# Moving low parts, modulation and the last rows' additions between the engines of a fused transformer layer

## The chip, the cores and the metric

The kernel runs on one core of a Trainium2 chip. Five engines work side by side, each through its own list of instructions in order: TensorE (PE, products; its weight loads are shown as PEld), VectorE (DVE), ScalarE (ACT), GpSimd (POOL) and SyncE (SP, which only issues transfers). ACT and POOL can issue transfers too. The metric is the time of one execution on the device in microseconds (us); less is better.

## The reference

One layer with latent tokens x (1024 x 1024), 256 context tokens, and adaLN modulation from a conditioning vector. Cut to what is computed:

```python
mod = silu(c) @ w_ada + b_ada                 # shift, scale, gate of both sub-layers
h = modulate(rms_norm(x, g_pre_mix), sh_m, sc_m)          # the context likewise
u_f, q_a, kv_a, kr_raw = split(h @ w_in)                  # 512, 256, 128, 32 columns
attn = mla_attention(q, k, v)      # from rms_norm(q_a) @ w_q_b, rms_norm(kv_a) @ w_kv_b, rotary parts
four = fourier_mix(u_f, w_fourier) # real 2-D DFT over positions and channels, then a map per group
x = x + gt_m * rms_norm(concat(four, attn) @ w_out, g_post_mix)
h2 = modulate(rms_norm(x, g_pre_ffn), sh_f, sc_f)
x = x + gt_f * rms_norm((silu(h2 @ w_gate) * (h2 @ w_up)) @ w_down, g_post_ffn)
```

All of it is in float32.

## The kernel before

**Products.** A float32 product is made of three products of a shorter type: each operand is split into a high part (a rounded copy) and a low part (what the copy leaves), and high x high, high x low and low x high are added up (`mm3_steps`, L68 to L70). `split` (L45) writes the high part on ACT (L50) and the low part on DVE (L56, "v") or on GpSimd (L58, "p"). Every operand that is split in the kernel passes through one ACT instruction and one DVE or GpSimd instruction of the same size.

**Order.** The kernel is written as one program; a tile scheduler sorts the instructions of each engine by when it thinks their inputs are there, and gives buffers in the order of the program. Where a few instructions are pinned (`pin`), their written order is kept. The order on an engine is so a result of the whole program, and can change where nothing is edited.

**Stages.** Constants (L167): 83 rows of 128 (c, c_ctx, gains, b_ada) are loaded and transposed into `cols`. `first_tiles` (L217): for each of eight slices j of the channels, a *set*, it loads the slice of w_ada (`araw`, 1 MB in two loads), splits it in two halves (`ah`, `al`, 128x1024 each), multiplies it with the conditioning vectors (16 products `aps`, L253 and L254), copies the result row (`arow`, L256), turns it into columns (`cps`, L259), forms `SH` and `A` (L261, L262), modulates two transposed tiles of x (`h`, L264), splits `h` (`hh`, `hl`), and adds 12 products with the slice of `w_in` to two accumulators (L290). The slice of w_in (`wraw`, 128x928) is split into `win`. The program puts modulation j + 2 ahead of the products of j. The tiles of x come through `normed` (L198): load (L202, two slots `xs`), square with sum (L86), rstd (L76, L78 on GpSimd), scaling in place on GpSimd (L204), then eight transposes on PE (L209). The third tile's transposes stand inside the last sets. `other_tiles` then takes the other tiles of x and the context: `h` for eight slices by ACT (L321, in a group of five and one of three around a split), products L345.

The Fourier stage (DFT over positions and channels) carries the weights of the attention beside it: `attention_weights` (L546) scales w_q (two tiles, 128x1024), w_k and w_v by gains and splits them (`wqh` and `wql`, and so on), splits the compressed keys (`kvTh`, `kvTl`) and the rotary keys `kr32` (32x1280) into K0. The first tile of w_q is scaled on GpSimd (L575) and split with its low part there; the second goes through `weight` (L567 on ACT scales into the high part, L568 on DVE makes the low part in one instruction). `wfpair`, `chh` and `chl` are the parts of w_fourier and the channel table; the products `mps` make a map from them, which is split into `map0` and `map1`.

After attention, output projection, gate and up, `down` (L1112) ends the kernel. Eight rows of 128 tokens finish one after the other: PE's last products of a row come into a bank, DVE adds them (L1190), ACT takes the square sum (L86) and adds the first half's (L1210), GpSimd raises to the power -1/2 (`rstd`, L1212). `finish` (L1164) is called for the row before: for rows 0 to 6 DVE multiplies by rstd and the gate row `Gf` (L1170), and GpSimd issues a store that adds to what lies in the output (x1, written there earlier); for row 7 x1 is loaded into a tile ahead of time, Gf is multiplied in early (L1205, L1209), DVE multiplies by rstd and adds x1 in halves (L1175), and the halves are stored plainly from SP and ACT (L1176).

## Time and profile before

| | |
|---|---|
| median of 3 runs | 1302.64 us (1301.27 to 1303.33) |
| profiled run | 1300.21 us |
| its span | 1298.4 us |
| granted clock, mean | 0.982 |
| PE busy | 1222.3 us, 94% |
| PEld (weight loads, beside PE) | 955.1 us, 74% |
| DVE busy | 934.2 us, 72% |
| ACT busy | 633.5 us, 49% |
| POOL busy | 479.4 us, 37% |
| chain that ended last | PE 49%, ACT 2%, POOL 2%, DVE 1%, DMA 1% |
| loaded and stored | 181.64 MB, 140 GB/s over the span |

Times in the trace are microseconds from the start of the span. The profiled run is one execution; its own time is the span and 1.8 us around it. A busy PE isn't a PE at its peak: products are pipelined, and their ends are modelled. Idle time ahead of an instruction is put down to what ended it, in brackets, by the last of its semaphores.

### The profile page before, as it was taken

Reading aid. Unit: us, or ns where it says so; the run is one execution under the profiler, and the core shown is the slowest. Engines: PE = TensorE matmul, PEld = TensorE weight load, DVE = VectorE, ACT = ScalarE, POOL = GpSimd, SP = SyncE. Lnnn points to the kernel's source line nnn. Section 1 sums busy time; section 2 is a strip of 40 time slices with the busy share of each in tenths; the row PEclk is TensorE's granted clock in tenths of the full one; section 3 lists DMA queues with packets and bytes.
Section 4 is the critical chain, followed back from the end, with each engine's and each line's share of the span. In section 5 each row is a group of like instructions: output and inputs, shape, how many; then the busy total and the mean of one; then the engine's idle time right before and its main releaser. Section 6 shows DMA issues by size and latency. Waiting matters only on the chain.

```text
span 1298.4 us, 15437 instructions
## 1 busy us (share of the span) xinstructions
PE 1222.3 (94%) x5474; PEld 955.1 (74%) x5474; DVE 934.2 (72%) x1301; ACT 633.5 (49%) x1045; POOL 479.4 (37%) x333
## 2 busy tenths in 40 slices
PE   5899978979999999889999999999999999999995
PEld 4588866756666666668788888888888887888884
DVE  6866586687675765353689887777777875898795
ACT  5467747646757668255644444433444433221232
POOL 4365556434555453253263332333311300000173
PEclk9999989989999999999999999999999999999998
DMA  8375211011110104642125554434454468987537
GB/s 318 127 246 169 69 49 36 31 33 46 38 33 17 34 18 139 179 140 101 60 81 179 178 178 149 150 110 144 163 178 154 153 212 335 344 296 256 194 130 130
DMA packets 79369, 181.64 MB, mean 140 GB/s; under 512 B 9569, under 2 KB 41332, under 8 KB 79292
## 3 DMA queue, kind: packets, MB, share of 16 engines
q1 hardware_dynamic: 67228, 137.89, 31.8%
q10 hardware_dynamic: 10800, 39.06, 7.7%
q0 software_dynamic: 1264, 3.70, 1.8%
q8 instruction: 43, 0.70, 0.2%
q14 instruction: 34, 0.28, 0.1%
HBM read 129.15 MB, written 51.48 MB: 139 GB/s over the span
## 4 chain that ended last, share of the span: by engine, by line
PE 49%; issue 2%; ACT 2%; POOL 2%; DVE 1%; DMA 1%; POOLq 0%; DVEq 0%; SPq 0%; ACTq 0%
PE gu L69 10%; PE gu L70 10%; PE gu L68 10%; PE y L774 5%; PE dn L68 4%; PE dn L70 4%; PE dn L69 4%; DMA unit<-zu 1%; DMA raw<-w_down 1%; POOL T L58 0%; POOL out_dram L1171 0%; PE T L209 0%; ACT H L321 0%; POOL rstd L1212 0%; DVE rows L1170 0%
## 5 line engine op out<-in xcount | busy, mean ns | idle before, releaser
L50 ACT ACTIVATE unit<-raw 128x512 fp32r<-128x512 f32 x171 | 105.5, 629 | 226.2 <-PE gu L70 106.3
L58 POOL TENSOR_TENSOR pl<-p,ph 128x1024 fp32r<-128x1024 f32 x53 | 128.8, 2431 | 148.0 <-ACT ph L50 111.6
L56 DVE TENSOR_TENSOR unit<-raw,unit 128x512 fp32r<-128x512 f32 x171 | 149.3, 881 | 27.3 <-ACT unit L50 26.9
L715 DVE TENSOR_REDUCE mx<-sps 128x1 f32<-128x512 f32 (+1 forms) x192 | 105.5, 594 | 31.5 <-PE sps L714 30.6
L640 ACT ACTIVATE p<-S 128x1024 f32<-128x1024 f32 x80 | 81.7, 1022 | 87.1 <-PE S L637 76.6
L935 POOL TENSOR_TENSOR s<-raw 128x512 f32<-128x512 f32 x22 | 33.8, 1537 | 241.4 <-DMA raw<-w_gate 167.9
L1155 POOL TENSOR_TENSOR rows<-rows,acc 128x512 f32<-128x512 f32 x8 | 13.5, 1705 | 212.8 <-DVE acc L1138 211.5
L50 ACT ACTIVATE ph<-p 128x1024 fp32r<-128x1024 f32 x80 | 84.3, 1057 | 1.9
L69 PE MATMUL gu<-T,unit 128*128 128x512 f32 x176 | 69.4, 394 | 0.9 <-POOL T L58 0.9
L70 PE MATMUL gu<-Bh,unit 128*128 128x512 f32 x176 | 69.4, 394 | 0.5 <-DVE unit L56 0.5
L68 PE MATMUL gu<-Bh,unit 128*128 128x512 f32 x176 | 69.4, 394 | 0.0
L69 PE MATMUL gu<-Bl,unit 128*128 128x512 f32 x176 | 69.3, 394 | 0.0
L70 PE MATMUL gu<-T,unit 128*128 128x512 f32 x176 | 69.3, 393 | 0.0
L68 PE MATMUL gu<-T,unit 128*128 128x512 f32 x176 | 69.2, 393 | 0.0
L68 PE MATMUL dn<-unit 128*128 128x512 f32 x148 | 58.2, 393 | 0.4 <-ACT unit L50 0.4
L70 PE MATMUL dn<-unit 128*128 128x512 f32 x148 | 58.0, 392 | 0.0
L69 PE MATMUL dn<-unit 128*128 128x512 f32 x148 | 58.0, 392 | 0.0
L621 PE MATMUL O<-pl,Vh 128*65 128x512 f32 x160 | 53.3, 403 | 4.6 <-POOL pl L58 3.8
L345 PE MATMUL acc<-win,hh 128*128 128x512 f32 (+1 forms) x224 | 55.8, 368 | 0.9 <-ACT hh L50 0.6
L1083 DVE TENSOR_TENSOR u<-u,gu 128x512 f32<-128x512 f32 x66 | 44.8, 681 | 15.6 <-PE gu L70 15.0
L78 POOL TENSOR_TENSOR rstd<-var,mhalf 128x1 f32<-128x1 f32 x44 | 27.6, 629 | 76.3 <-DVE var L76 75.6
L774 PE MATMUL y<-woh,xth 128*128 128x512 f32 x128 | 52.5, 410 | 2.4 <-ACT xth L50 2.4
(425 smaller groups left out, 3552.9 us busy)
## 6 DMA issues: line engine op xcount, KB each, us to landing
zu<-zpair ACTq DMA_DIRECT2D x50, 512.0 KB, 4.3
unit<-zu SPq DMA_DIRECT2D x47, 512.0 KB, 4.6
adraw<-w_ada SPq DMA_DIRECT2D x32, 512.0 KB, 3.9
units<-zu SPq DMA_DIRECT2D x27, 512.0 KB, 5.5
zu<-zone ACTq DMA_DIRECT2D x24, 512.0 KB, 3.1
raw<-w_gate SPq DMA_DIRECT2D x22, 512.0 KB, 4.2
raw<-w_up SPq DMA_DIRECT2D x22, 512.0 KB, 6.3
raw<-w_down SPq DMA_DIRECT2D x22, 512.0 KB, 5.2
```

The lines of the kernel that those rows point to most:

```text
L50: nc.scalar.activation(hi, src, AF.Copy)
L56: self.lastv = nc.vector.tensor_tensor(lo, src, hi.bitcast(F32), ALU.subtract)
L58: nc.gpsimd.tensor_tensor(lo, src, hi.bitcast(F32), ALU.subtract)
L68: self.nc.tensor.matmul(out, ah, bh, start=i == 0, stop=False)
L69: self.nc.tensor.matmul(out, ah, bl, start=False, stop=False)
L70: self.nc.tensor.matmul(out, al, bh, start=False, stop=i == n - 1)
L345: nc.tensor.matmul(acc[:, o], a[:, k, :], b[:, k, c], start=k == 0 and n == 0, stop=k == KT - 1 and n == 2)
L621: nc.tensor.matmul(O[0:m, ns], a, b[:, ns], start=k == 0 and i == 0, stop=k == NK - 1 and i == 2)
L640: nc.scalar.activation(p32, S, AF.Exp, scale=SCALE)
L715: nc.vector.tensor_reduce(mx[:, i, c:c + 1], ps[:, 0:n], AX.X, ALU.max)
L774: nc.tensor.matmul(ps[:, ns], u[:, k, :], w[:, k, ns], start=k == 0 and i == 0, stop=k == KT - 1 and i == 2)
L1083: V(d, d, ps, ALU.add)
```

## The change

- `normed` takes a queue; the first two tiles of x are loaded from ACT's queue instead of SP's. The third and later tiles stay on SP.
- In `first_tiles` the low part of w_in goes from GpSimd to DVE; the copy `arow` and the modulation `h` go from DVE to ACT.
- In the Fourier stage the low parts of w_fourier, the channel table and the rotary keys go from GpSimd to DVE; the first tile of w_q goes through `weight`, as the second does, so that the scaling on GpSimd (L575) is gone.
- The rows of constants are padded with zeros from 83 to 96.
- At the end x1 is loaded ahead for rows 4 to 7 (four loads instead of one). For these rows the product with Gf is made on DVE into accumulators that are free by then (L1193 of the changed kernel), DVE multiplies by rstd and adds x1 in one instruction, and the store is plain, from SP (row 7 in halves, from SP and ACT). Rows 0 to 3 keep the adding store of GpSimd. `finish` is called after the power of the row instead of before it.

```diff
--- before.py
+++ after.py
@@ -167,7 +167,7 @@
     def constants(self):
         tc, nc, t, cst = self.tc, self.nc, self.t, self.cst
         rows = cst.tile([P, P], F32, name="rows")
-        nc.sync.dma_start(rows[0:NROWS, :], t["rows"])
+        nc.sync.dma_start(rows[0:96, :], t["rows"])
         self.ident = cst.tile([P, P], F32, name="ident")
         nc.sync.dma_start(self.ident, t["ident"])
         self.comb = cst.tile([4, 2], F32, name="comb")
@@ -195,11 +195,11 @@
         self.Gm = cst.tile([P, D], F32, name="Gm")
 
 
-    def normed(self, src):
+    def normed(self, src, queue=None):
 
         nc = self.nc
         xs = self.xp.tile([P, D], F32, name="xs", bufs=2)
-        nc.sync.dma_start(xs, src)
+        (queue or nc.sync).dma_start(xs, src)
         r = self.rstd(self.xp, self.meansq(self.xp, xs, D))
         nc.gpsimd.tensor_scalar(xs, xs, r, 0.0, ALU.mult, ALU.add)
         return xs
@@ -228,10 +228,10 @@
             raw = sw.tile([P, 928], F32, name="wraw", bufs=3)
             nc.sync.dma_start(raw, t["w_in"][j * P:(j + 1) * P, :])
             wh, wl = (w[:, j, :] for w in self.win)
-            self.split(wh, wl, raw, "a", "p")
+            self.split(wh, wl, raw, "a", "v")
             return wh, wl
         xT = sw.tile([P, KT, 2 * P], F32, name="xT")
-        xs = [self.normed(t["x"][i * P:(i + 1) * P, :]) for i in range(2)]
+        xs = [self.normed(t["x"][i * P:(i + 1) * P, :], nc.scalar) for i in range(2)]
         raw = ada_load(0)
         nc.sync.dma_start(self.comb, t["comb"])
         for i in range(2):
@@ -253,7 +253,7 @@
                 nc.tensor.matmul(ps[0:4, 0:256], self.c4[:, k, :], ah[:, k, :], start=k == 0, stop=False)
                 nc.tensor.matmul(ps[0:4, 0:256], self.c4[:, k, :], al[:, k, :], start=False, stop=k == KT - 1)
             row = sw.tile([4, 256], F32, name="arow", bufs=2)
-            nc.vector.tensor_copy(row, ps[0:4, 0:256])
+            nc.scalar.activation(row, ps[0:4, 0:256], AF.Copy)
             ps = self.bankB("cps")
             for i in range(2):
                 nc.tensor.matmul(ps[:, 2 * i:2 * i + 2], row[:, i * P:(i + 1) * P], self.comb, start=True, stop=True)
@@ -261,7 +261,7 @@
             nc.vector.tensor_scalar(self.SH[:, :, j], ps[:, 0:2], self.cols[:, b0:b0 + 1], None, ALU.add)
             nc.vector.tensor_scalar(self.A[:, :, j], ps[:, 2:4], self.b1[:, 8 + j:9 + j], self.cols[:, R_GPM + j:R_GPM + j + 1], ALU.add, ALU.mult)
             h = sw.tile([P, 2 * P], F32, name="h", bufs=2)
-            nc.vector.tensor_scalar(h, xT[:, j, :], self.A[:, 0, j:j + 1], self.SH[:, 0, j:j + 1], ALU.mult, ALU.add)
+            nc.scalar.activation(h, xT[:, j, :], AF.Identity, bias=self.SH[:, 0, j:j + 1], scale=self.A[:, 0, j:j + 1])
             hh = sw.tile([P, 2 * P], F32R, name="hh", bufs=3)
             hl = sw.tile([P, 2 * P], F32R, name="hl", bufs=3)
             self.split(hh, hl, h, "a", "v")
@@ -521,8 +521,8 @@
         pair = fp.tile([P, 2, 512], F32R, name="wfpair")
         wfh, wfl = pair[:, 0, :], pair[:, 1, :]
         chh, chl = (fp.tile([P, 2, P], F32R, name=f"ch{x}") for x in "hl")
-        self.split(wfh, wfl, wf, "a", "p")
-        self.split(chh, chl, ch, "a", "p")
+        self.split(wfh, wfl, wf, "a", "v")
+        self.split(chh, chl, ch, "a", "v")
         run(positions(0))
         self.last_turn(bank)
         run(weights)
@@ -568,16 +568,11 @@
             nc.vector.scalar_tensor_tensor(w[1], raw, self.cols[:, g:g + 1], w[0].bitcast(F32), ALU.mult, ALU.subtract)
         weight(self.wk, rawk, R_GKV)
         for k in range(2):
-            w = [w[:, k, :] for w in self.wq]
-            if k:
-                weight(w, raws[k], R_GQ + k)
-            else:
-                nc.gpsimd.tensor_scalar(raws[k], raws[k], self.cols[:, R_GQ + k:R_GQ + k + 1], 0.0, ALU.mult, ALU.add)
-                self.split(*w, raws[k], "a", "p")
+            weight([w[:, k, :] for w in self.wq], raws[k], R_GQ + k)
             self.split(*(x[:, k, :] for x in self.qT), self.q32[:, k, :], "a", "v")
         yield
         self.split(*self.kvT, self.kv32, "a", "v")
-        self.split(kh[64:96, :], kl[64:96, :], self.kr32[64:96, :], "a", "p")
+        self.split(kh[64:96, :], kl[64:96, :], self.kr32[64:96, :], "a", "v")
         weight(self.wv, rawv, R_GKV)
         yield
 
@@ -910,8 +905,8 @@
             for j in range(2):
                 for p in group:
                     yield self.raw((p, "w", j), t["w_down"][(2 * p + j) * P:(2 * p + j + 1) * P, :])
-        i = NT - 1
-        yield self.raw(("x1", i), t["out"][i * P:(i + 1) * P, :])
+        for i in range(NT // 2, NT):
+            yield self.raw(("x1", i), t["out"][i * P:(i + 1) * P, :])
 
     STEPS = [(m, i) for ms in ((1, 2), (6, 5), (7,), (3,), (4,)) for m in ("w_gate", "w_up") for i in ms]
     DOWN = (1, 2, 6, 5, 7, 3, 4)
@@ -1158,7 +1153,9 @@
         last = NF // 2 - 1
         ss = {}
         pin = self.tc.keep_in_program_order
-        rows = [x[:, q].rearrange("p h c -> p (h c)") for x in (up, low) for q in range(4)]
+
+        rows = [up[:, q].rearrange("p h c -> p (h c)") for q in range(4)]
+        rows += [a[n][:, q:q + 2].rearrange("p q c -> p (q c)") for n in (6, 1) for q in (0, 2)]
         pending = []
 
         def finish():
@@ -1166,12 +1163,12 @@
             while pending:
                 i, r = pending.pop()
                 where = t["out"][i * P:(i + 1) * P, :]
-                if i + 1 < NT:
+                if i < NT // 2:
                     pin(nc.vector.scalar_tensor_tensor(rows[i], rows[i], r, self.Gf, ALU.mult, ALU.mult))
                     nc.gpsimd.dma_start(where, rows[i], accum_op=ALU.add)
                     continue
                 xs = self.raws["x1", i][1]
-                for cs in (slice(0, 512), slice(512, D)):
+                for cs in [slice(0, 512), slice(512, D)] if i + 1 == NT else [slice(0, D)]:
                     pin(nc.vector.scalar_tensor_tensor(xs[:, cs], rows[i][:, cs], r, xs[:, cs], ALU.mult, ALU.add))
                     (nc.scalar if cs.start else nc.sync).dma_start(where[:, cs], xs[:, cs])
 
@@ -1192,7 +1189,8 @@
                     i = q + 4 * zh
                     c = a[n][:, q, :]
                     s = self.meansq(f1, c, D, 512)
-                    final = i + 1 == NT
+                    if zh:
+                        pin(V(rows[i][:, cs], c, self.Gf[:, cs], ALU.mult))
                     v = f1.tile([P, 1], F32, name="var", bufs=16)
                     if first:
                         ss[i] = v
@@ -1201,15 +1199,11 @@
                             for l, add in (5, V), (4, G):
                                 x = a[l][:, q, :]
                                 pin(add(x, x, a[7][:, q, :], ALU.add))
-                        if final:
-                            pin(V(c, c, self.Gf[:, cs], ALU.mult))
                     else:
-                        finish()
-                        if final:
-                            pin(V(c, c, self.Gf[:, cs], ALU.mult))
                         nc.scalar.activation(v, s, AF.Identity, bias=ss[i])
                         r = f1.tile([P, 1], F32, name="rstd", bufs=4)
                         pin(nc.gpsimd.tensor_tensor(r, v, self.mhalf[:, 0:1], ALU.pow))
+                        finish()
                         pending.append((i, r))
             if n != 5:
                 self.unit_done(*((p, m, n) for p in group for m in "zw"))
@@ -1257,7 +1251,8 @@
         "w_fourier": a["w_fourier"][0], "w_out": a["w_out"][0], "w_gate": a["w_gate"][0], "w_up": a["w_up"][0], "w_down": a["w_down"][0],
         "b_ada_rows": a["b_ada"].reshape(6, D), "g_post_mix": a["g_post_mix"].reshape(1, D), "g_post_ffn": a["g_post_ffn"].reshape(1, D),
     }
-    arrays["rows"] = np.concatenate([a[k].reshape(-1, P) for k in ("c", "c_ctx", "g_pre_mix", "g_pre_ffn", "b_ada", "g_q_a", "g_kv_a")])
+    rows = np.concatenate([a[k].reshape(-1, P) for k in ("c", "c_ctx", "g_pre_mix", "g_pre_ffn", "b_ada", "g_q_a", "g_kv_a")])
+    arrays["rows"] = np.concatenate([rows, np.zeros((96 - NROWS, P), rows.dtype)])
 
     arrays["w_ada_mix"] = arrays["w_ada"][:, :2 * D].reshape(KT, P, 2, KT, P).transpose(3, 1, 0, 2, 4)
```

The lines below are the order of instructions on one engine: line, operation, output<-inputs, shape, and a count where several follow each other. Behind the edits, lines of the changed kernel have numbers lower by up to 7.

ACT at the end of the first stage, from the last split of `win` on, before (`xs` are tiles of x, L86 their squares, L321 the modulation of the next tile):

```order
L50 ACTIVATE win_102<-wraw 128x928
L50 ACTIVATE hh<-h 128x256
L86 ACTIVATE junk,ss<-xs 128x1024 x2
L50 ACTIVATE hh<-h 128x256
L321 ACTIVATE h<-xT,SH,A 128x128 x5
L50 ACTIVATE hh<-h 128x512
L321 ACTIVATE h<-xT,SH,A 128x128 x3
```

And now:

```order
L50 ACTIVATE win_102<-wraw 128x928
L264 ACTIVATE h<-xT,SH,A 128x256
L50 ACTIVATE hh<-h 128x256
L86 ACTIVATE junk,ss<-xs 128x1024
L256 ACTIVATE arow<-aps 4x256
L86 ACTIVATE junk,ss<-xs 128x1024
L264 ACTIVATE h<-xT,SH,A 128x256
L50 ACTIVATE hh<-h 128x256
L86 ACTIVATE junk,ss<-xs 128x1024
L321 ACTIVATE h<-xT,SH,A 128x128 x5
```

ACT has the h of the last sets and the last arow in its list, and a third square of a tile of x stands ahead of the five L321.

DVE at the weights of the Fourier stage, before (`kvTl` is the low part of the compressed keys, `zl` of a Fourier block):

```order
L56 TENSOR_TENSOR kvTl<-kv32T,kvTh 128x1280
L568 SCALAR_TENSOR_TENSOR wql<-wqraw,cols,wqh 128x1024
L568 SCALAR_TENSOR_TENSOR wvl<-wkraw,cols,wvh 128x512
L56 TENSOR_TENSOR zl<-po,zh 128x2x256
L56 TENSOR_TENSOR zl<-pm,zh 128x2x128
```

And now:

```order
L56 TENSOR_TENSOR kvTl<-kv32T,kvTh 128x1280
L568 SCALAR_TENSOR_TENSOR wql<-wqraw,cols,wqh 128x1024 x2
L56 TENSOR_TENSOR K0l<-kr32T,K0h 32x1280
L56 TENSOR_TENSOR wfpair<-wfraw,wfpair 128x512
L56 TENSOR_TENSOR chl<-wfraw,chh 128x256
L568 SCALAR_TENSOR_TENSOR wvl<-wkraw,cols,wvh 128x512
L56 TENSOR_TENSOR zl<-po,zh 128x2x256
```

Four low parts that GpSimd made stand in DVE's list, three of them between wql and wvl.

GpSimd at the end, from the adding store of row 2 on, before:

```order
L1171 DMA out_dram<-rows_9078 128x1024
L1212 TENSOR_TENSOR rstd<-var,mhalf 128x1
L1171 DMA out_dram<-rows_9078 128x1024
L1212 TENSOR_TENSOR rstd<-var,mhalf 128x1
L1171 DMA out_dram<-rows_9079 128x1024
L1212 TENSOR_TENSOR rstd<-var,mhalf 128x1
L1171 DMA out_dram<-rows_9079 128x1024
L1212 TENSOR_TENSOR rstd<-var,mhalf 128x1
L1171 DMA out_dram<-rows_9079 128x1024
L1212 TENSOR_TENSOR rstd<-var,mhalf 128x1
```

And now, from the first power on:

```order
L1205 TENSOR_TENSOR rstd<-var,mhalf 128x1 x2
L1168 DMA out_dram<-rows_9077 128x1024
L1205 TENSOR_TENSOR rstd<-var,mhalf 128x1
L1168 DMA out_dram<-rows_9077 128x1024
L1205 TENSOR_TENSOR rstd<-var,mhalf 128x1
L1168 DMA out_dram<-rows_9077 128x1024
L1205 TENSOR_TENSOR rstd<-var,mhalf 128x1
L1168 DMA out_dram<-rows_9077 128x1024
L1205 TENSOR_TENSOR rstd<-var,mhalf 128x1 x3
```

A row's power stands ahead of the store of the row before it, and the last three powers have no store between them.

DVE over the last two rows now (`acc` are the accumulators that take the product with Gf, `raw` the tiles of x1):

```order
L1187 TENSOR_TENSOR rows_9078<-rows_9078,dn 128x512
L1193 TENSOR_TENSOR acc_9074<-rows_9078,Gf 128x512
L1172 SCALAR_TENSOR_TENSOR raw<-acc_9075,rstd,raw 128x1024
L1187 TENSOR_TENSOR rows_9078<-rows_9078,dn 128x512
L1193 TENSOR_TENSOR acc_9074<-rows_9078,Gf 128x512
L1172 SCALAR_TENSOR_TENSOR raw<-acc_9074,rstd,raw 128x1024
L1172 SCALAR_TENSOR_TENSOR raw<-acc_9074,rstd,raw 128x512 x2
```

A row's addition and its product with Gf stand ahead of the multiplication of the row before, which adds x1.

## Rows read from the trace of the kernel before

**Rows 1.** Window: us, busy (instructions) of PE, PEld, DVE, ACT, POOL, PEclk, DMA, GB/s

```profile
160.00:180.00 20.00, 12.40 (x53) 8.83 (x52) 16.19 (x22) 12.84 (x21) 9.85 (x5) 0.91 0.11 29
```

**Rows 2.** Timeline, PE, first stage: start, duration, engine, line, operation, [idle before <-releaser]

```profile
21.43 1.42 PE L290 MATMUL acc<-win,hh 128*128 128x512 f32 x6
...
53.12 0.28 PE L254 MATMUL aps<-al,c 128*4 128x256 f32 x1 [1.39 <-DVE al L56]
...
60.00 0.28 PE L254 MATMUL aps<-al,c 128*4 128x256 f32 x1 [1.57 <-DVE al L56]
...
65.53 1.08 PE L290 MATMUL acc<-win,hh 128*128 128x512 f32 x4
...
67.71 0.58 PE L290 MATMUL acc<-win,hl 128*128 128x512 f32 x2
69.38 1.06 PE L209 MATMUL xT<-ident,xs 128*128 128x128 f32 x8 [1.08 <-ACT h L321]
70.42 1.11 PE L345 MATMUL acc<-win,hh 128*128 128x512 f32 x4
```

**Rows 3.** Timeline, DVE, first stage

```profile
55.51 1.22 DVE L56 TENSOR_TENSOR al<-araw,ah 128x1024 fp32r<-128x1024 f32 x1
...
56.83 3.12 DVE L56 TENSOR_TENSOR al<-araw,ah 128x1024 fp32r<-128x1024 f32 x1
...
60.76 0.43 DVE L56 TENSOR_TENSOR hl<-h,hh 128x256 fp32r<-128x256 f32 x1 [0.48 <-ACT hh L50]
```

**Rows 4.** Timeline, ACT and POOL, first stage

```profile
53.74 1.99 ACT L50 ACTIVATE ah<-araw 128x1024 fp32r<-128x1024 f32 x2
...
56.68 2.19 POOL L58 TENSOR_TENSOR win<-wraw,win 128x928 fp32r<-128x928 f32 x1 [4.70 <-ACT win L50]
```

**Rows 5.** SP's queue at x's loads; DMA issues (count, KB each, median us to landing)

```profile
41.77 24.40 SPq L202 DMA_DIRECT2D xs<-x  x3
...
adraw<-w_ada SPq DMA_DIRECT2D x32, 512.0 KB, 3.9
...
xs<-x SPq DMA_DIRECT2D x16, 512.0 KB, 6.8
```

**Rows 6.** Timeline, Fourier stage, DVE and PE

```profile
161.43 1.49 DVE L56 TENSOR_TENSOR kvTl<-kv32T,kvTh 128x1280 fp32r<-128x1280 f32 x1 [0.61 <-ACT kvTh L50]
164.85 1.99 DVE L568 SCALAR_TENSOR_TENSOR wql<-wqraw,cols,wqh 128x1024 fp32r<-128x1024 f32 x1 [1.93 <-ACT wqh L567]
166.77 2.83 DVE L568 SCALAR_TENSOR_TENSOR wvl<-wkraw,cols,wvh 128x512 fp32r<-128x512 f32 x1
...
172.40 0.69 DVE L699 TENSOR_TENSOR tq<-qps,ropeq 32x512 f32<-32x512 f32 x1
...
169.10 0.50 PE L70 MATMUL qps<-qTh,wql 128*128 128x512 f32 x1 [4.29 <-POOL wql L58]
...
178.21 0.49 PE L70 MATMUL Sp<-zh,map1l 128*128 128x512 f32 x1 [2.19 <-DVE map1l L56]
```

**Rows 7.** Timeline, the last rows: PE, DVE, ACT, POOL

```profile
1281.16 0.39 PE L70 MATMUL dn<-units,unit 128*128 128x512 f32 x1
...
1283.88 0.39 PE L70 MATMUL dn<-units,unit 128*128 128x512 f32 x1
...
1286.20 0.68 DVE L1190 TENSOR_TENSOR rows<-rows,dn 128x512 f32<-128x512 f32 x1
1288.09 1.28 DVE L1170 SCALAR_TENSOR_TENSOR rows<-rows,rstd,Gf 128x1024 f32<-128x1024 f32 x1 [1.22 <-POOL rstd L1212]
...
1291.18 1.42 DVE L1175 SCALAR_TENSOR_TENSOR raw<-rows,rstd,raw 128x512 f32<-128x512 f32 x2 [1.21 <-POOL rstd L1212]
...
1287.72 0.29 ACT L1210 ACTIVATE var<-ss,var 128x1 f32<-128x1 f32 x1
...
1289.67 0.89 POOL L1171 DMA_DIRECT2D out_dram<-rows  x1 [1.62 <-DVE rows L1170]
1290.29 0.86 POOL L1212 TENSOR_TENSOR rstd<-var,mhalf 128x1 f32<-128x1 f32 x1
```

## The prediction

> **What bounds the kernel now.** I read the table of windows first, then TensorE's (PE's) own rows with the idle time in front of them, then the rows of the engine each idle time is put down to. PE is busy nearly throughout, and what it loses lies in three places that the change touches.
>
> In the first stage PE takes a set (16 products for the modulation, 12 for two tiles of x) from 53.12 to 60.00, 6.88 us, and the last 1.57 of these it waits for al from VectorE (DVE) [rows 2]. DVE's al takes 1.22 us, but 3.12 where GpSimd (POOL) makes a low part of win beside it (56.68 to 58.87) [rows 3, 4]: DVE is slowed by an engine that shares the work with it.
>
> In the Fourier stage PE waits 4.29 us at 169.10 for wql of GpSimd and 2.19 at 178.21 for DVE's map1l; the window 160 to 180 has PE busy 12.40 of 20 and a granted clock of 0.91 [rows 1, 6].
>
> At the end PE stops at 1283.88 + 0.39, yet the last multiplication starts at 1291.18 [rows 7]. The rows 5 to 7 run in a loop: an L1170 on DVE releases an accumulating store on GpSimd (1289.67), the power for the next row's rstd stands behind it (1290.29) although its var is there at 1287.72 + 0.29, and the next DVE multiplication waits 1.2 for that power. One turn is 1291.18 - 1288.09 = 3.09 us, while PE delivers a row each 1283.88 - 1281.16 = 2.72.
>
> The profiled run took 1300.21 (span 1298.4, 1.8 around it); the median of the runs is 1302.64, 2.4 above. I sum differences in the trace and subtract them from the median. A difference of 0.2%, 2.6 us, is about what a measurement can tell from none.
>
> **First stage.** PE's own need for a set is 6.88 - 1.57 = 5.31. What would the others need? DVE keeps two al (2.44), a low part of win (928/1024 of 1.22: 1.1), hl (0.43), SH and A (two short ones, no more than 0.43 each): 4.8 at most. ScalarE (ACT) gets h and arow beside two ah (1.99 for both), win's high part (0.9) and hh: 1.99 + 0.9 + 3 x 0.43 = 4.2 [rows 3, 4]. GpSimd has nothing left in the loop, so al should stay at 1.22. PE becomes the bound with 5.31.
>
> The first product L290 stands at 21.43. It depends on arow, which DVE copied behind an al; on ACT it waits for no al, worth between nothing and one al (1.22): I take 0.7, so 20.7. x's own queue moves two issues from SP's front to ACT's; this I count within that 0.7. [...]
>
> Six sets of 5.31 follow, then two without modulation work, each 67.71 + 0.58 - 65.53 = 2.76, and the transposes of the third x tile, 1.06: 20.7 + 31.9 + 5.5 + 1.1 = 59.2, against 67.71 + 0.58 = 68.3 now [rows 2]. The stage's products end 9.1 earlier.
>
> Not all of it arrives at the next stage. The next tile of x can be loaded only when the transposes have freed one of two slots: SP stands 24.40 us at its three loads, from 41.77 to 66.2 [rows 5]. And in the new order on ACT the square of that tile (L86) stands ahead of the five L321 that the second transposed tile releases. Now the transposes stand ahead of one set (65.53), in the new order ahead of two. They end at 59.2 - 5.5 = 53.7. The load is issued at +0.3, lands after 3.9 (the 32 like loads of w_ada; the 16 loads of x show 6.8, waits for a slot in it, which I keep as the upper bound), and its square takes 1.2 (an ah's 1.0 and a short read of the sum): 59.1. From there as now from 65.53 to 69.38, 3.85, to the transposes, and 1.04 more to the first L345: 64.0. PE would be idle for 3.8 between, where it is 1.08 now. [...] After a wait of 3.8 I take 1.0 (0 to 1.8). L345 then starts at 65.0 instead of 70.42: **-5.5**, with bounds -9.1 (no give-back) and -1.1 (landing 6.8 and all of the clock, start unchanged).
>
> **Fourier weights.** DVE is through kvTl at 161.43 + 1.49 = 162.9 and waits for wqh until 164.85; then wql takes 1.99 and wvl 2.83, both beside GpSimd [rows 6]. Uncontended, 128x1024 takes 1.28 and 128x512 0.68 [rows 7], and an instruction starts 0.07 before the last one's end (166.77 against 164.85 + 1.99) [rows 6]. DVE's new list up to tq: two wql 2.56, K0l 1.49 (as long a row as kvTl), wfpair, wvl and a first zl 0.68 each, chl and two zl 0.43 each, three K0l together as one of 128x1024 and a half, 1.9: 9.3, less 11 overlaps of 0.07, 8.5. From 162.9 that is 171.4; tq is at 172.40 now. wql is there some 4 us earlier, so PE's 4.29 goes, but behind tq the same DVE chain to map1l at 178.21 follows, and PE waits there instead: the 2.19 grows by nearly all it has saved ahead. What arrives is DVE's 1.0: **-1.1** with the shorter clock loss, from 0 (a longer list, or wqh late as now) to -2.
>
> **The end.** The new list per row on DVE is an add (0.68), a product with Gf (0.68) and a multiplication with x1 (1.28): 2.64 and less with overlaps, under PE's 2.72. Add 7 then starts when PE is done, 1284.3, not 1286.20. From its end (1284.95) the square, var and power take what they take now, 1287.72 + 0.29 - 1286.88 = 1.1 and 0.86; no store is ahead of the power. So rstd is ready at 1287.0, DVE's row 6 is done at 1286.8, and the last multiplication starts at 1287.0 instead of 1291.18: **-4.2**, bounds -3.4 (row 6's store delays row 7's) and -5. The three more loads of x1 lie in a stage where PE's products stand without a gap; they cost nothing as long as SP's weight loads stay ahead of PE, and a landing like x's, 6.8, if not. 96 rows of input instead of 83 are priced at nothing: the load lies ahead of x's and w_ada's, which PE waits for; without that cover, a few tenths.
>
> Sum: -5.5 - 1.1 - 4.2 = -10.8. 1302.64 - 10.8 = **1291.8**. Between the three places PE is the bound, so what one gains isn't taken by the next.
>
> **The rivals.**
> 1. No give-back at the handover: the tile of x lands in time or another order hides it. For it: its load could be issued with a slot free by then. Then the first term is -9.1: 1288.2. 20%.
> 2. A larger one: x lands after 6.8, all of the 1.8 of clock is lost. First term -5.5 + 2.9 + 0.8 = -1.8: 1295.5. For it: the median 6.8 of x's loads. 13%.
> 3. The end does not do what it says: row 7's halves wait for row 6's plain store on the same engines, a transfer like w_ada's 3.9, so only some 0.7 is left: 1295.3. Against it: the same bytes as now, spread earlier. 5%.
> 4. Slower. ACT works in order, and now stands in the chain of every set: half an ah 1.0, al 1.22, last product 0.28, arow 0.43, cps and A some 0.9, h and hh 0.86, 4.7; the other ah and win, 1.9, come behind: 6.6. If PE, in order too, stands in both tiles' products (2.76) when arow is ready, a set takes 9.3, six sets lose 14.5, and with the other terms the time is 1302.64 + 14.5 - 5.3 = 1311.8. It decides from a set of 7.8. Against it: the new order puts arow one set behind its ah, so that the chain spreads over two sets. 8%, of which 2 within 0.2%.
>
> **How the numbers follow.** My forecast has 54%. The range takes in rivals 1 to 3 and the price ends of the three terms: 1286.5 to 1297. Outside are rival 4, and some 6% of larger gains and 5% of rivals 2 and 3 together. Faster by over 0.2%: 0.91; within 0.2%: 0.03; slower: 0.06.
>
> **What would show it.** First stage: al at 1.2 everywhere, sets at 5.3, L290 ending near 59. Handover: an idle time of 3 to 5 us on PE ahead of the second transposes, put down to ACT's h, with L86 ahead of it; no such wait is rival 1. Fourier: no wait for wql, but a longer one for map1l. End: no wait of DVE on rstd over 0.5, the last multiplication within 3 us of PE's last product. The forecast is wrong if a set still takes over 6.5, ACT being the releaser (rival 4), or if the time from the last multiplication to the end grows over 7 us (rival 3).

## The result: 1286.4 us, 1.2% faster, and where the time went

The changed kernel takes 1286.36 us (median of 4 runs, 1284.79 to 1289.26) against 1301.95 for the kernel before (4 runs, three of them those of the table ahead of the prediction): a ratio of 0.9884, interval 0.9861 to 0.9907. The forecast was 1291.8, with 1286.5 to 1297. The median lies 0.14 below that range; the ratio, applied to the 1302.64 that the forecast set out from, gives 1287.5, inside it. The profiled run took 1286.13, its span is 1284.4 (1298.4 before), granted clock 0.984 (0.982). The direction and the three places were right; the gain was 15.6 by the medians, 15.1 by the ratio, 14.0 by the spans, not 10.8.

Times of the same points in both traces, in us:

| point | before | now | difference |
|---|---|---|---|
| first L290 | 21.43 | 22.38 | +0.95 |
| last L290 ends | 68.29 | 58.72 | -9.57 |
| first L345 | 70.42 | 63.46 | -6.96 |
| first kps product | 161.80 | 153.56 | -8.24 |
| first sps product | 178.64 | 169.46 | -9.18 |
| last product (dn) | 1283.88 | 1275.12 | -8.76 |
| last multiplication on DVE | 1291.18 | 1278.59 | -12.59 |
| end of the span | 1298.4 | 1284.4 | -14.0 |

Each column is one execution. The five kernels of this study with the first stage of before have their first L290 at 21.41 to 22.33 and their first L345 at 70.42 to 70.75, once at 72.56.

**First stage.** The groups of DVE instructions between 20 and 58 us (count, busy us, mean ns), now:

```profile
L56 DVE TENSOR_TENSOR al<-araw,ah 128x1024 fp32r<-128x1024 f32 x12 | 14.5, 1219 | 1.2 <-ACT ah L50 1.1
L56 DVE TENSOR_TENSOR win<-wraw,win 128x928 fp32r<-128x928 f32 x7 | 7.8, 1116 | 0.0
```

and before:

```profile
L56 DVE TENSOR_TENSOR al<-araw,ah 128x1024 fp32r<-128x1024 f32 x12 | 21.6, 1800 | 0.0
```

Every al takes 1.2 us now. DVE does more, and is through earlier. PE's timeline at the end of the stage, which answers to [rows 2]:

```profile
22.38 0.82 PE L290 MATMUL acc<-win,hh 128*128 128x512 f32 x3
...
52.64 1.03 PE L209 MATMUL xT<-ident,xs 128*128 128x128 f32 x8
...
58.14 0.58 PE L290 MATMUL acc<-win,hl 128*128 128x512 f32 x2
61.87 1.94 PE L209 MATMUL xT<-ident,xs 128*128 128x128 f32 x8 [3.15 <-ACT h L321]
63.46 1.78 PE L345 MATMUL acc<-win,hh 128*128 128x512 f32 x4
```

No wait for al is left, and the wait ahead of the second L209 has grown from 1.08 to 3.15. ACT's timeline and SP's issue show why: the square (L86) of a tile whose load was issued only at 53.74 stands ahead of L321.

```profile
57.27 1.06 ACT L86 ACTIVATE junk<-xs 128x1024 bf16<-128x1024 f32 x1 [3.97 <-DMA xs<-x]
58.24 0.19 ACT L86 ACTIVATION_READ_ACCUMULATOR junk<-xs 128x1 f32 x1
58.33 1.83 ACT L321 ACTIVATE h<-xT,SH,A 128x128 f32<-128x128 f32 x5
...
53.74 0.33 SPq L202 DMA_DIRECT2D xs<-x  x1
```

**Fourier weights.** DVE and PE, which answer to [rows 6]:

```profile
154.61 2.48 DVE L568 SCALAR_TENSOR_TENSOR wql<-wqraw,cols,wqh 128x1024 fp32r<-128x1024 f32 x2
163.12 0.70 DVE L694 TENSOR_TENSOR tq<-qps,ropeq 32x512 f32<-32x512 f32 x1
...
160.98 0.79 PE L68 MATMUL mps<-wfpair,chh 128*128 128x512 f32 x1 [2.52 <-DVE zl L56]
168.86 0.79 PE L70 MATMUL Sp<-zh,map1l 128*128 128x512 f32 x1 [3.54 <-DVE map1l L56]
```

The wait of 4.29 for wql is gone, and 2.52 ahead of mps and 3.54 ahead of map1l (2.19 before) stand for it. The way from the first kps to the first sps fell from 16.84 to 15.90.

**The end**, which answers to [rows 7]:

```profile
1275.12 0.39 PE L70 MATMUL dn<-units,unit 128*128 128x512 f32 x1
...
1276.88 1.28 DVE L1172 SCALAR_TENSOR_TENSOR raw<-acc,rstd,raw 128x1024 f32<-128x1024 f32 x1
1278.59 1.41 DVE L1172 SCALAR_TENSOR_TENSOR raw<-acc,rstd,raw 128x512 f32<-128x512 f32 x2 [0.44 <-POOL rstd L1205]
...
1277.52 1.04 POOL L1205 TENSOR_TENSOR rstd<-var,mhalf 128x1 f32<-128x1 f32 x1 [1.68 <-ACT var L1203]
```

The last multiplication stands 3.5 us behind PE's last product, start to start (7.3 before), and the end 5.8 behind that (7.2).

### The profile page after: what moved, and what is told of

It is laid out like the page before. It is cut to its first block, busy times and chain, and to the rows that moved or that the text cites. A ratio compares the mean times of both kernels' runs of the same rounds, so it can differ in the third digit from the quotient of the medians.

```text
span 1284.4 us, 15451 instructions
## 1 busy us (share of the span) xinstructions
PE 1220.7 (95%) x5474; PEld 956.0 (74%) x5474; DVE 923.5 (72%) x1303; ACT 639.0 (50%) x1061; POOL 451.5 (35%) x317
## 4 chain that ended last, share of the span: by engine, by line
PE 52%; DMA 1%; ACT 1%; issue 1%; DVE 1%; POOL 1%; POOLq 0%; DVEq 0%; SPq 0%; ACTq 0%
PE gu L69 10%; PE gu L70 10%; PE gu L68 10%; PE y L769 6%; PE dn L68 5%; PE dn L70 5%; PE dn L69 5%; DMA unit<-zu 1%; DMA raw<-w_down 1%; POOL T L58 0%; PE T L209 0%; ACT H L321 0%; ACT unit L50 0%; DVE unit L56 0%; ACT T L50 0%
## 5 line engine op out<-in xcount | busy, mean ns | idle before, releaser
L345 PE MATMUL acc<-win,hh 128*128 128x512 f32 (+1 forms) x224 | 55.0, 364 | 0.6 <-ACT hh L50 0.6
```

Of the source, the lines that this page charges most:

```text
L345: nc.tensor.matmul(acc[:, o], a[:, k, :], b[:, k, c], start=k == 0 and n == 0, stop=k == KT - 1 and n == 2)
```

## Experiments on the first stage: which edit, and what GpSimd costs DVE

The theory was that GpSimd's low part of win slows DVE; the rival that DVE's queue is too long. Each edit alone, and both without x's queue.

```diff
-            self.split(wh, wl, raw, "a", "p")
+            self.split(wh, wl, raw, "a", "v")
```

> The kernel before, with one edit: the low part of win on DVE instead of GpSimd. Theory (GpSimd beside DVE is the cost): al takes 1.2 us everywhere instead of 3.1 in every set; DVE has 2.44 + 1.1 + 0.43 + 0.4 + h and arow 0.8 = 5.2 a set, so a set takes 5.3 to 5.6 instead of 6.9, the last L290 ends at 60 to 61.5 (before 68.3). A square of the next x tile stands ahead of the five L321 in this kernel too, so 2 to 3.5 of it are given back; the time is 4 to 6 us less than before, 1296 to 1298. Rival (the queue of DVE is the cost, arow and h standing behind al): arow and h still stand there, a set stays over 6.3 and the time within 3 us of before.

```diff
-            nc.vector.tensor_copy(row, ps[0:4, 0:256])
+            nc.scalar.activation(row, ps[0:4, 0:256], AF.Copy)
-            nc.vector.tensor_scalar(h, xT[:, j, :], ...)
+            nc.scalar.activation(h, xT[:, j, :], AF.Identity, ...)
```

> The kernel before, with one edit: arow and h on ACT instead of DVE; win's low part stays on GpSimd. Theory (GpSimd beside DVE): an al still takes some 3.1 us in every set, a set takes 6 us or more, the last L290 ends after 64, the gain is 2 to 4 us. Rival (DVE's queue): arow no longer waits for al, a set falls to 5.5 or less, the last L290 ends before 62, the gain is 6 us or more.

Both of these diffs together:

> The kernel before, with both edits of the first stage: win's low part on DVE, arow and h on ACT; x stays on SP's queue. Theory: a set takes 5.0 to 5.3, the first L290 stands at 20.5 to 21.5 and the last ends at 57 to 58.5; no square of the next x tile stands ahead of the five L321 in this kernel, so the first L345 follows within 2.3 us, at 59 to 61 (before 70.4): 9 to 11 us less than before. Rival (the two edits overlap, and the better one alone gives all): not over 1 us faster than the better of the two single edits.

Measured (a set: from the first L290 to the end of the last, less 6.6 for two sets without modulation and the transposes, over six):

| kernel | first L290 | a set | last L290 ends | wait ahead of second L209 | first L345 | median | ratio to before |
|---|---|---|---|---|---|---|---|
| before | 21.43 | 6.7 | 68.29 | 1.08 | 70.42 | 1300.55 | |
| win's low part on DVE | 23.10 | 5.05 | 59.99 | 3.38 | 64.41 | 1293.95 | 0.9951 (0.9934 to 0.9967) |
| arow and h on ACT | 19.28 | 6.05 | 62.15 | 0.88 | 64.08 | 1294.79 | 0.9950 (0.9931 to 0.9969) |
| both | 21.03 | 4.95 | 57.34 | 0.24 | 58.62 | 1287.88 | 0.9898 (0.9878 to 0.9917) |
| changed kernel | 22.38 | 4.96 | 58.72 | 3.15 | 63.46 | 1286.36 | 0.9884 (0.9861 to 0.9907) |

Ratios here and below are to runs of the kernel before made beside the kernel in question; they aren't quotients of the medians shown. The first edit alone did what the theory says and somewhat more (a set of 5.05 for 5.3 to 5.6, a gain of 6.6 for 4 to 6). Both together gave 12.7 us, more than the 9 to 11 expected, and are no overlap of one cause. The second did more than the theory allowed (al was to stay at 3.1, the gain at 2 to 4), and that is the more instructive run. GpSimd and DVE in it:

```profile
36.18 2.19 POOL L58 TENSOR_TENSOR win<-wraw,win 128x928 fp32r<-128x928 f32 x1 [3.58 <-ACT win L50]
...
36.44 2.21 DVE L56 TENSOR_TENSOR hl<-h,hh 128x256 fp32r<-128x256 f32 x1 [0.71 <-ACT hh L50]
38.58 1.21 DVE L56 TENSOR_TENSOR al<-araw,ah 128x1024 fp32r<-128x1024 f32 x1
```

Here al takes 1.2, and hl, 0.43 alone, takes 2.21: it started 0.26 behind GpSimd's instruction and ended 0.28 behind its end. In [rows 3, 4] al started 0.15 behind GpSimd's and ended 1.08 behind its end, nearly its own length. So DVE is not slowed by a factor: 3.12 is 2.6 times the 1.22 of al, 2.21 is 5 times the 0.43 of hl. Both end as if the instruction that came second had stood still until the other's was over: the price, 1.90 on al and 1.78 on hl, is nearly what was left of GpSimd's 2.19 when it started (2.04 and 1.93). Why, no trace here shows. With this price on hl instead of al, DVE has time for it, and PE waits some 0.5 a set for hl instead of 1.5 for al.

x's queue alone, with DVE and GpSimd sharing the work as before:

```diff
-        xs = [self.normed(t["x"][i * P:(i + 1) * P, :]) for i in range(2)]
+        xs = [self.normed(t["x"][i * P:(i + 1) * P, :], nc.scalar) for i in range(2)]
```

> The kernel before, with one edit: the first two tiles of x on ACT's queue. Theory (the queue costs by the orders it brings): the second square stands behind an ah on ACT, the first L290 stands later than 21.4, at 22 to 23; at the end of the stage three squares stand ahead of the five L321, the next tile's load stands there in the way, PE waits 2.5 to 4 us instead of 1.1 for its transposes, and the first L345 stands at 72 to 75 (70.4): 2 to 4 us more than before, 1302.5 to 1305. Rival (landing earlier helps): the first L290 at 20 to 21, the time 0.5 to 1.5 us less, 1299 to 1300.

Measured 1300.20 against 1299.75, ratio 1.0009 (0.9991 to 1.0027): neither theory. The first L290 stands at 29.17, much later than either said, yet the last one ends at 64.07 and the first L345 stands at 68.92. GpSimd and DVE in the loop:

```profile
40.82 2.62 POOL L58 TENSOR_TENSOR win<-wraw,win 128x928 fp32r<-128x928 f32 x1 [2.50 <-ACT win L50]
45.95 2.62 POOL L58 TENSOR_TENSOR win<-wraw,win 128x928 fp32r<-128x928 f32 x1 [2.50 <-ACT win L50]
...
40.20 1.20 DVE L56 TENSOR_TENSOR al<-araw,ah 128x1024 fp32r<-128x1024 f32 x1
41.73 0.22 DVE L261 TENSOR_SCALAR SH<-cps,cols 128x2 f32<-128x2 f32 x1 [0.33 <-PE cps L259]
41.87 0.27 DVE L262 TENSOR_SCALAR A<-cps,b,cols 128x2 f32<-128x2 f32 x1
42.18 1.42 DVE L264 TENSOR_SCALAR h<-xT,A,SH 128x256 f32<-128x256 f32 x1
```

The same instructions on the same engines take 5.13 us a set here (40.82 to 45.95) and 6.88 in the set of [rows 2]. Part of the late start is work done earlier: 48 of the modulation products stand ahead of the first L290 here, 33 before. Now al comes first and GpSimd's instruction, which starts 0.58 ahead of al's end, takes 2.62 instead of 2.19; SH and A, which read `cps` from PSUM, run beside GpSimd at their usual 0.22 and 0.27, and only h pays, 1.42 instead of 0.40. What decides is which instruction meets which, and moving an issue at the program's start changed that.

## Experiments on x's queue and the handover

The changed kernel with x on SP's queue (the diff above reversed), and the changed kernel with that one square held behind L321 on ACT:

> The changed kernel with x's first tiles back on SP's queue, nothing else. Theory (x's own queue costs, since with it ACT's list puts the second square behind an ah, and at the end of the stage a square that waits for its load ahead of L321): the first L290 stands at 21.0 instead of 22.4, PE waits 1.1 instead of 3.2 for the next tile, the first L345 stands 3 us earlier, at 60 to 61 instead of 63.5, and the time is 2 to 4 us less than that of the changed kernel, 1282.5 to 1284.5. Rival (the queue helps, the tiles land earlier): the first L290 is later than 22.4 and the time is the same or longer, 1286 to 1288.

```diff
+            self.hold = self.tc.keep_in_program_order if n == 0 else (lambda i: i)
+            if n == 0:
+                nxt = self.front(...)
             if n + 2 < len(todo):
                 self.xs.append(self.normed(...))
```

(`hold` goes around the instructions of L86 and L321, and `front`, which makes tile 3's L321, is written ahead of tile 4's load and square.)

> The changed kernel (x on ACT's queue) with one place of the order held: the square of the third late tile of x (tile 4) stands behind the L321 of tile 3 on ACT instead of ahead of them. Theory (the handover's give-back is this square's wait for its load): PE's wait ahead of the second transposes falls from 3.15 us to under 1.1, the first L345 stands at 60 to 61 instead of 63.5, the time is 2 to 3.5 us less than the changed kernel's, 1283 to 1284.5; the first L290 stays at 22.4, so some 1 us of the gain of x on SP's queue is missing. Rival (the wait moves to the next tile, whose square is late now): a wait of 2 us or more stands ahead of the third transposes, and the time stays within 1 us of 1286.4.

| kernel | first L290 | wait ahead of second L209 | first L345 | median | ratio to before |
|---|---|---|---|---|---|
| changed kernel | 22.38 | 3.15 | 63.46 | 1286.36 | 0.9884 (0.9861 to 0.9907) |
| x on SP's queue | 21.27 | 0.24 | 60.86 | 1281.48 | 0.9851 (0.9836 to 0.9865) |
| square held back | 22.91 | none | 59.88 | 1282.37 | 0.9866 (0.9844 to 0.9888) |

PE at the second transposes with x on SP's queue, and with the square held back (lines of this kernel have numbers higher by up to 5):

```profile
59.82 1.06 PE L209 MATMUL xT<-ident,xs 128*128 128x128 f32 x8 [0.24 <-ACT h L321]
60.86 1.10 PE L345 MATMUL acc<-win,hh 128*128 128x512 f32 x4
```

```profile
59.09 1.03 PE L210 MATMUL xT<-ident,xs 128*128 128x128 f32 x8
59.88 1.08 PE L350 MATMUL acc<-win,hh 128*128 128x512 f32 x4
```

Holding one instruction back removed the wait (part of it comes back one tile later, 1.84 us ahead of the third L209, for GpSimd's scaling). So the give-back was that square's wait for its load. The three kernels with that square ahead of L321 (win's low part alone, x's queue alone, the changed kernel) wait 3.15 to 3.38 there, those without it at most 1.1. x on SP's queue removes it, since ACT's list then has the square behind L321, and it starts 1.1 earlier as well, both as expected: 1281.48, 1 us under what was expected, is the best of the study. The two were not timed against the changed kernel itself; by their ratios to before they are 0.2 to 0.3% ahead of it, with intervals that touch or overlap.

The padded rows belong to the queue. The first use of the rows on ACT, before (83 rows, x on SP):

```profile
4.80 0.31 ACT L178 ACTIVATE rows<-rows 16x128 f32<-16x128 f32 x1 [2.79 <-DMA rows<-rows]
```

with x's queue alone (83 rows, x on ACT):

```profile
7.67 0.31 ACT L178 ACTIVATE rows<-rows 16x128 f32<-16x128 f32 x1 [4.75 <-DMA rows<-rows]
```

in the changed kernel (96 rows, x on ACT; ACT itself is free only at 2.95):

```profile
3.96 0.31 ACT L178 ACTIVATE rows<-rows 16x128 f32<-16x128 f32 x1 [1.01 <-DMA rows<-rows]
```

and with x back on SP (96 rows):

```profile
2.57 0.31 ACT L178 ACTIVATE rows<-rows 16x128 f32<-16x128 f32 x1 [0.56 <-DMA rows<-rows]
```

83 rows are there 2.9 us later when x's tiles are issued at the same time, 96 rows 1.4 later, and still ahead of the 83 rows of before. Why, no run here shows. Without the queue the padding brings nothing to PE: the first L290 stands at 21.27 with it and at 21.04 without (a kernel below). How much of the late start with x's queue alone (29.17) is due to the 83 rows is open, since no run has the queue and 96 rows and nothing else.

## Experiments on the end

The order on GpSimd alone; the whole edit alone; and the new end for rows 6 and 7 only, on the kernel before and on the changed one with x on SP.

```diff
-                        finish()
...
                         pin(nc.gpsimd.tensor_tensor(r, v, self.mhalf[:, 0:1], ALU.pow))
+                        finish()
```

> The kernel before, with one edit: at the end a row's power is issued on GpSimd ahead of the store of the row before it (finish after the power); all rows but the last keep the adding store. Theory (the place of the power behind the store is the cost): a row needs 0.68 + 1.28 on DVE, under PE's 2.72, and the last L1175 starts 3.1 to 3.8 us behind PE's last product instead of 7.3; from it to the end 6 to 7.2 as before, since the adding store of row 6 is still there: 3 to 4.5 us less than before, 1296.5 to 1299. Rival (the adding stores are the cost): the loop stays over 3 us a row, the last L1175 starts over 6 us behind PE's last product, the gain is under 1.5 us.

All of the change's edits in `all_loads` and `down`, and nothing else:

> The kernel before, with the whole edit of the end: four x1 tiles loaded ahead, Gf and x1 on DVE and plain stores for rows 4 to 7, the power ahead of the store. Theory: the last multiplication starts 3.5 us behind PE's last product (7.3 before), and the end follows it within 6 (7.2 before): 5 to 5.5 us less than before, 1295 to 1297. If the order on GpSimd is the whole of it, the difference to the kernel with the order alone is under 0.7; if the plain stores shorten the way to the end, 1 to 1.5.

```diff
-        for i in range(NT // 2, NT):
+        for i in range(NT - 2, NT):
```

(This is the list of x1 loads; the same bound stands in `finish` and ahead of the product with Gf.)

> The kernel before with the new end for rows 6 and 7 alone: two x1 tiles loaded ahead, Gf and x1 on DVE and plain stores for these two, the power ahead of the store; rows 0 to 5 keep the adding store. Theory (the 16 DMA engines are full at the end: an adding store of 512 KB moves at 200 GB/s, 2.6 us, a plain one at 400, 1.3): 6 x 2.6 + 2 x 1.3 = 18.2 us of transfers instead of 7 x 2.6 + 1.3 = 19.5 with the order alone, so the end lies 11 to 12 us behind PE's last product (12.85 with the order alone, 8.4 with four plain rows): 1295 to 1298. Rival (the last adding store's own way, some 9 us from issue to end): row 5's is issued as PE ends, so the end lies 9 to 9.5 us behind PE's last product: 1294 to 1296.

> The changed kernel with x on SP's queue and the new end for rows 6 and 7 alone (83 rows of input as before). Theory (full DMA engines at the end): the end lies 11 to 12 us behind PE's last product instead of 8.4, so 2.5 to 3.5 us more than with four plain rows, 1284 to 1285. Rival: within 1 us of it, 1281 to 1282.5.

| kernel | rows with an adding store | PE's last product to last multiplication | PE's last product to the end | median | ratio to before |
|---|---|---|---|---|---|
| before | 7 | 7.30 | 14.5 | 1300.44 | |
| power ahead of the store | 7 | 3.77 | 12.9 | 1298.59 | 0.9995 (0.9983 to 1.0007) |
| rows 6 and 7 new | 6 | 3.50 | 9.7 | 1295.40 | 0.9963 (0.9945 to 0.9982) |
| whole new end | 4 | 3.48 | 8.4 | 1294.26 | 0.9949 (0.9934 to 0.9964) |
| changed kernel, x on SP | 4 | 3.47 | 8.4 | 1281.48 | 0.9851 (0.9836 to 0.9865) |
| the same, rows 6 and 7 new | 6 | 3.50 | 9.9 | 1283.17 | 0.9867 (0.9840 to 0.9895) |

The first experiment overturned my account of the end. With the power ahead of the store the last multiplication comes 3.5 us earlier against PE, as forecast, but the end only 1.6, and the time doesn't move by anything that can be measured. PE's last product, row 6's adding store and the last multiplication in that kernel:

```profile
1283.15 0.39 PE L70 MATMUL dn<-units,unit 128*128 128x512 f32 x1
...
1287.30 0.89 POOL L1171 DMA_DIRECT2D out_dram<-rows  x1 [1.08 <-DVE rows L1170]
...
1286.92 1.41 DVE L1175 SCALAR_TENSOR_TENSOR raw<-rows,rstd,raw 128x512 f32<-128x512 f32 x2
```

The windows of its last microseconds (the last three columns: granted clock, mean busy share of the 16 DMA engines, GB/s) follow; its PE ends at 1283.5:

```profile
1284.00:1286.00 2.00, 0.00 (x0) 0.00 (x0) 1.15 (x3) 1.01 (x3) 0.67 (x2) 1.00 1.05 203
1286.00:1288.00 2.00, 0.00 (x0) 0.00 (x0) 2.00 (x3) 0.00 (x0) 0.92 (x2) 1.00 1.01 190
1288.00:1290.00 2.00, 0.00 (x0) 0.00 (x0) 0.33 (x1) 0.00 (x0) 0.19 (x1) 0.52 1.07 197
1290.00:1292.00 2.00, 0.00 (x0) 0.00 (x0) 0.00 (x0) 0.00 (x0) 0.00 (x0) 0.50 0.90 181
1292.00:1294.00 2.00, 0.00 (x0) 0.00 (x0) 0.00 (x0) 0.00 (x0) 0.00 (x0) 0.50 0.66 183
```

and of the kernel with the whole new end, whose PE ends at 1284.2:

```profile
1282.00:1284.00 2.00, 2.00 (x10) 1.46 (x8) 1.97 (x3) 1.02 (x3) 0.56 (x1) 1.00 0.99 203
1284.00:1286.00 2.00, 0.15 (x1) 0.00 (x0) 1.85 (x4) 1.00 (x3) 0.49 (x1) 1.00 1.02 399
1286.00:1288.00 2.00, 0.00 (x0) 0.00 (x0) 1.56 (x3) 0.02 (x1) 1.04 (x1) 1.00 0.48 193
1288.00:1290.00 2.00, 0.00 (x0) 0.00 (x0) 0.65 (x1) 0.00 (x0) 0.00 (x0) 0.86 1.01 385
1290.00:1292.00 2.00, 0.00 (x0) 0.00 (x0) 0.00 (x0) 0.00 (x0) 0.00 (x0) 0.50 0.17 64
```

With the order alone the DMA engines are busy without a break until some 9 us behind PE, at 181 to 203 GB/s, and row 7's plain halves move among the adding stores. Row 6's adding store is issued only 4.15 us behind PE's last product and lands 7.0 later (the median of the seven is 6.4): that is 11.2 of the 12.9. With the whole new end the plain stores move at 385 to 399 GB/s at the same busy share, and the engines are not full to the end: from 1286 to 1288 their mean busy share is 0.48. What had been issued is through by then, row 6's plain store is issued only at 1286.83, and the end follows the last multiplications again. So the earlier multiplication counts only where no adding stores stand in its way. Added in this order, 4.5 us of the new end's 6.1 (14.5 to 8.4) come with the stores, 1.6 with the order.

A busy share near 1 doesn't show by itself that no more can be moved. In the kernel before it is 0.96 to 1.15 from 1284 to 1292 as well, at 156 to 199 GB/s.

The size for one row isn't settled. Two plain rows instead of one (7 to 6 adding) were worth 3.2 us to the end, where the rates alone gave 0.9 to 1.9 and the rival 3.4 to 3.9. But row 5's adding store, the last in that kernel, lands 5.3 us after its issue and 3.7 ahead of the end, so the rival's reason does not fit either. On the changed kernel with x on SP the end comes 9.9 us behind PE with two plain rows, where 11 to 12 was expected. The runs show that the adding stores are the cause, not whether their rate or the last store's own way has the larger part. On top of the other edits two plain rows and four could not be told apart by the times.

## Experiments on the Fourier weights

The edit alone, and the changed kernel with x on SP but without this edit (and with 83 rows):

```diff
-        self.split(wfh, wfl, wf, "a", "p")
+        self.split(wfh, wfl, wf, "a", "v")
...
-                self.split(*w, raws[k], "a", "p")
+            weight([w[:, k, :] for w in self.wq], raws[k], R_GQ + k)
```

> The kernel before, with the edit of the Fourier weights alone. Theory (the wait goes from wql to map1l): the wait of 4.3 us for wql is gone, waits of 2.5 and 3.5 stand at mps and map1l instead, and the way from the first kps to the first sps product is 15.8 to 16 us instead of 16.84: 1 us less than before, within the measurement's noise (1298 to 1301). Rival (the wait is saved): the way is under 14.5 and the time 2.5 us less or better.

> The changed kernel with x on SP's queue, without the edits of the Fourier weights and of the 96 rows. Theory (that edit is worth 1 us): 0.5 to 2 us more than the kernel with it, 1282 to 1283.5. Rival (more of the Fourier stage runs at the lower clock with the edit, granted clock 0.69 in 160 to 180 there against 0.86 without it, which eats the gain): the same or less, 1279.5 to 1281.5.

Alone: 1300.56 against 1300.44, ratio 0.9998 (0.9986 to 1.0010). The way from kps to sps is 15.87 us (16.84 before): the theory's 1 us, which is below what times can tell. Over all traces it is 15.87 to 15.90 in the five kernels with the edit and 16.75 to 17.34 in the nine without. In the second pair 1283.94, ratio 0.9872 (0.9855 to 0.9889), against 1281.48 with the edit; the way is 16.80 against 15.88. That is 2.5 us by the medians in favour of the edit, more than the trace shows, with intervals that overlap: only the 0.9 us of the way is shown. It was measured at a lower granted clock. The window of this way, before and in the changed kernel:

```profile
161.80:178.64 16.84, 9.24 (x33) 5.84 (x31) 14.18 (x17) 10.11 (x17) 8.51 (x4) 0.90 0.02 5
```

```profile
153.56:169.46 15.90, 9.15 (x33) 5.73 (x32) 15.01 (x21) 9.97 (x17) 0.14 (x1) 0.83 0.05 15
```

PE is busy about as long in both, but at a granted clock of 0.83 now against 0.90 (0.74 to 0.83 in the five kernels with the edit, 0.80 to 0.90 in the nine without). Before, the granted clock of this way is 0.50 in one stretch, seen from 170 to 172, behind the wait of 4.29; now in two, seen from 161 to 163 and from 168 to 169, around the ends of the waits of 2.52 and 3.54.

## Why the prediction was right, and where not

**What bounds the kernel.** The three places were the right ones, and between them PE carried the gains on.

**First stage: right.** The last L290 was to end 9.1 us earlier, and ended 9.6. Two errors in it cancel: the start came 0.95 later, not 0.7 earlier, and a set fell to 4.96, not 5.31. The 5.31 (53.12 to 58.43) has no other wait in it. But 0.16 of it is the end of its last products, which the next set overlaps, and the 6.6 taken off for the last two sets and the transposes is more than the 6.1 that they take now (52.64 to 58.72); the six sets ahead of them take 5.06 each (22.26 to 52.64). x's queue was to save up to 0.7 at the start; the four kernels with x on SP and both edits of the first stage start at 21.03 to 21.51, the two with x on ACT at 22.38 and 22.91. A start as before, 21.4, would have come nearer than my 20.7. The cost goes with the order on ACT, where the second square stands behind an ah; no run here has the queue without that order.

**Handover: right in kind.** 3.15 us of idle time with L86 ahead of L321, against a forecast of 3.8; the load was there a little earlier (its square starts at 57.27; 53.7 + 0.3 + 3.9 = 57.9 was forecast). The forecast charged 1.0 for the clock ahead of L345, and rival 2 charged 1.8; no run shows either as a term of its own. What the trace shows is a granted clock of 0.52 from 61.87 to 65.08, behind the idle time (1.00 from 56 to 60), with the transposes at 1.94 for 1.06 and the first products at 1.78 for 1.11: from the second transposes to the third group of L345 3.62 us passed, 2.41 before. L345 stood 7.0 earlier, not 5.5, and at the third group of L345 6.3 (65.49 against 71.79).

**Fourier: right.** -0.94 against -1.1, and the wait went to map1l and mps. The 0.1 for a shorter clock loss is shown by no run: the granted clock of this way is lower now, 0.83 for 0.90.

**Between: not in the sum.** From the first L345 to kps 91.38 us passed before and 90.10 now, though no product there was edited. The windows of that stretch, before first:

```profile
70.42:161.80 91.38, 89.41 (x477) 79.00 (x477) 60.94 (x116) 63.68 (x176) 57.55 (x64) 0.98 0.49 160
```

```profile
63.46:153.56 90.10, 88.37 (x479) 78.06 (x478) 56.49 (x114) 62.14 (x171) 54.22 (x61) 0.99 0.48 148
```

The granted clock is 0.98 in the first and 0.99 in the second. The six kernels with 0.98 there take 91.0 to 92.0 us, the eight with 0.99 or 1.00 take 89.4 to 90.2 (91.5 with the square held back, which has the wait of 1.84 in it), and kernels with the code of before stand on both sides. So this 1.3 goes with the clock, not with an edit. The medians differ by more than the spans (15.6 against 14.0) because the profiled run of before was 1.7 below the median of its 4 runs, that of the changed kernel 0.2: that is scatter.

**The end: the size right, the reason not.** I forecast -4.2 from the last multiplication, and it came 3.8 earlier against PE. The step that failed is the tacit one, that the end follows that multiplication at a fixed distance: it followed in 7.2 us before, in 9.1 with the order alone, in 5.8 now. The adding stores of the rows ahead set it. The order alone, for which my sum would have given the same 4.2, moved the end by 1.6 against PE and gained nothing that times can tell. The end fell by 5.2 against PE because rows 4 to 7 stopped adding in the same edit. My rival 3 looked at stores too, but at row 6's plain one, the cheap kind. The three more loads of x1, priced at nothing, cost nothing: from the first sps to PE's last product 1104.4 us pass with the whole new end alone, 1105.2 before.

Rival 4 (ACT as the chain) did not happen: ACT's waits for the aps and for A did not lengthen a set. Rival 1 is what the kernels without the square ahead show.

## What to carry to other kernels

A DVE instruction on SBUF that met a GpSimd one in the first stage cost nearly what was left of the latter (1.90 of 2.04 us on al, 1.78 of 1.93 on hl); look at which pairs meet, since another order can be worth as much as another engine. Ahead of pricing the last instructions of a kernel, look at the DMA engines behind PE's last product, window by window: where they are busy without a break, an earlier last instruction may bring little (1.6 of 3.5 us here), and fewer or cheaper transfers more; where they were half idle (a busy share of 0.48 with the whole new end), the end followed the last multiplications. After moving a load to another queue, look for what the scheduler put ahead of what, at the start and where the next load of the same buffers is waited for.

## Not expected of the hardware

Adding stores kept the 16 DMA engines as busy as plain ones at half the rate (181 to 203 GB/s against 385 to 399), and in the kernel before as busy at 156 to 199. An 83-row load was there at 7.67 us beside two loads of 512 KB, 2.9 us later than without them, a 96-row load at 3.96, 1.4 later. DVE's short instructions on PSUM (0.22 and 0.27 us) ran beside a GpSimd instruction without loss, where hl and h, on SBUF alone, took 2.21 for 0.43 and 1.42 for 0.40.
